# One residual load in mid-run moved mostly to a chosen eleven of the 16 DMA engines, and 15 tiny reads removed, in a memory-bound layer norm

## The chip, the cores and the metric

The kernel runs on one core of a Trainium2 chip. The metric is the device time of one execution in microseconds (us). The profile counts the packets of every queue against the core's 16 DMA engines, which move data between HBM and the on-chip memory (SBUF, 128 partitions); transfers are issued on the sync queue, the scalar queue and GpSimd (queue tables below).

## The reference

```python
# x, residual: (16, 1024, 512) float32; gamma, beta: 512 values
z = x + residual
mean = np.mean(z, axis=-1, keepdims=True)
var = np.var(z, axis=-1, keepdims=True)
return gamma * (z - mean) / np.sqrt(var + eps) + beta
```

Two arrays of 33.5 MB are read and one is written, 100.7 MB in all. There are 16,384 rows; each partition holds 128 of them, and "row" below means one of these 128, across all partitions.

## The kernel before

GpSimd adds x and residual two rows at a time, ScalarE takes mean and variance, VectorE applies two passes. All large transfers go through the sync queue: loads of 8 rows (16 KB per partition), stores of 16 rows (32 KB per partition). A load or store of 128 partitions makes 128 packets, one for each partition (in the trace 4224 packets of 16 KB for 33 transfers of 8 rows), and 16 reports of its landing come, one for each engine; at equal shares that is 8 partitions on each engine.

```python
X_CHUNKS = [8] * 16
R_CHUNKS = [8] * 16
OUT_CHUNKS = [16] * 7 + [8, 4, 4]
Z_ROWS, R_ROWS, STORE_LAG = 64, 32, 40

def load_r(lo, n):
    nc.sync.dma_start(out=part(rbuf, R_ROWS, lo, n), in_=dram(rf, lo, n))
def store(lo, n):
    nc.sync.dma_start(out=dram(of, lo, n), in_=part(zbuf, Z_ROWS, lo, n))
# ... (adds, statistics, affine passes cut)

few = consts.tile([16, 16, 16], FP32)
probes = list(range(15, 0, -1))
def probe():                       # tiny reads of 15, 14, ... 1 rows of 64 bytes
    if probes and asked > 48:
        k = probes.pop(0)
        nc.sync.dma_start(out=few[:k, k, :], in_=xf[:k, :16])

for lo, n in spans(X_CHUNKS):
    asked = lo + n
    load_x(lo, n)
    probe()
    while loads_r and loads_r[0][0] + loads_r[0][1] <= asked:
        while added < loads_r[0][0] + loads_r[0][1] - R_ROWS:
            added, done = next(steps)
        load_r(*loads_r.pop(0))
        probe()
    # ... (broadcast of gamma and beta cut)
    store_due()
```

Of the kernel before, what the change touches and what calls it, by code (L numbers as in the profile page):

```python
# [7 lines left out]
FP32 = mybir.dt.float32  # L8
# [5 lines left out]


X_CHUNKS = [8] * 16
R_CHUNKS = [8] * 16
OUT_CHUNKS = [16] * 7 + [8, 4, 4]

GROUP = 2  # L20

Z_ROWS = 64
R_ROWS = 32
# [5 lines left out]
def kernel(  # L29
# [9 lines left out]
    nc = tc.nc  # L39
    P = nc.NUM_PARTITIONS  # L40
    xf = x.flatten_outer_dims()
    rf = residual.flatten_outer_dims()
    of = out.flatten_outer_dims()
    N, D = xf.shape
# [3 lines left out]
    def spans(sizes):  # L48

        assert sum(sizes) == total  # L50
        return [(sum(sizes[:c]), n) for c, n in enumerate(sizes)]
# [3 lines left out]
    def dram(t, lo, n):  # L55

        k = lo % BLOCK
        assert k + n <= BLOCK
        v = t[P * (lo - k) : P * (lo - k + BLOCK), :].rearrange("(p j) d -> p j d", p=P)
        return v[:, k : k + n, :].rearrange("p a b -> p (a b)")  # L60

    consts = ctx.enter_context(tc.tile_pool(name="consts", bufs=1))
# [14 lines left out]
    rbuf = consts.tile([P, R_ROWS, D], FP32)  # L77

    def part(buf, size, lo, n):
        assert lo % size + n <= size  # L80
        return buf[:, lo % size : lo % size + n, :].rearrange("p a b -> p (a b)")

    def load_x(lo, n):
        nc.sync.dma_start(out=part(zbuf, Z_ROWS, lo, n), in_=dram(xf, lo, n))  # L84

    def load_r(lo, n):
        nc.sync.dma_start(out=part(rbuf, R_ROWS, lo, n), in_=dram(rf, lo, n))  # L87

    def store(lo, n):
        nc.sync.dma_start(out=dram(of, lo, n), in_=part(zbuf, Z_ROWS, lo, n))  # L90
# [19 lines left out]
    groups = []  # L110
    for lo, n in spans(R_CHUNKS):
        for j in range(0, n, GROUP):
# [75 lines left out]
    def spread():  # L188
        for k, dest in ((0, gamma_t), (1, beta_t)):
            nc.tensor.matmul(dest, ones, gb_row[:, k, :], start=True, stop=True)  # L190
# [14 lines left out]
    added = done = asked = 0  # L205
    loads_r = spans(R_CHUNKS)
    stores = spans(OUT_CHUNKS)

    def store_due():
        nonlocal added, done  # L210
        while stores and (
            stores[0][0] + stores[0][1] <= asked - STORE_LAG or asked == total
        ):
            lo, n = stores.pop(0)
            while done < lo + n:
                added, done = next(steps)
            store(lo, n)


    few = consts.tile([16, 16, 16], FP32)  # L220
    probes = list(range(15, 0, -1))

    def probe():
        if probes and asked > 48:
            k = probes.pop(0)
            nc.sync.dma_start(out=few[:k, k, :], in_=xf[:k, :16])

    for lo, n in spans(X_CHUNKS):
        asked = lo + n
        assert not stores or stores[0][0] >= asked - Z_ROWS  # L230
        load_x(lo, n)
        probe()
        while loads_r and loads_r[0][0] + loads_r[0][1] <= asked:

            while added < loads_r[0][0] + loads_r[0][1] - R_ROWS:
                added, done = next(steps)
            load_r(*loads_r.pop(0))
            probe()
        if lo == 0:
            spread()  # L240
        store_due()
# [35 lines left out]
```

## Time and profile before

| | before |
|---|---|
| time, median of 3 | 243.33 us (243.16 to 243.63) |
| span of the profiled run | 241.5 us |
| data moved | 100.76 MB, mean 417 GB/s |
| GpSimd waiting for residual loads | 69.9 us |
| one packet of 16 KB / 32 KB / 8 KB | 611 / 1213 / 309 ns |

From the profile page of the kernel before: the mean busy share of the 16 DMA engines in 40 slices of the span (tenths), what they moved in GB/s in each slice, and the queue table (packets, MB, share of 16 engines' span).

```profile
DMA  7999999999999999999999999999999999999992
GB/s 261 434 434 434 432 427 421 426 419 434 432 449 434 404 429 426 434 425 422 434 430 437 434 426 430 429 442 418 432 421 422 470 400 430 470 434 434 399 410 109
q1 hardware_dynamic: 6288, 100.67, 97.9%
q14 instruction: 10, 0.08, 0.1%
```

The engines are busy from the first slice to the last, so their throughput is the bound. In the last slice, however, they are only two tenths busy on average. From the table of groups, the GpSimd adds (count | busy us, mean ns | idle us before them and what ended it):

```profile
L120 POOL TENSOR_TENSOR zbuf<-zbuf,rbuf 128x1024 f32<-128x1024 f32 x64 | 148.6, 2355 | 71.7 <-DMA rbuf<-in_residual_dram 69.9
```

GpSimd waits for data, not the reverse. The trace also records when each engine reports each transfer as landed. These are the reports of the last store, sorted (us from the start of the span; worked out from the semaphore records):

```
before: 236.78 236.78 236.79 236.81 236.83 236.83 236.90 236.91 236.93 236.95 237.06 237.07 | 237.51 239.25 240.11 240.33
```

Twelve engines finish together near 237, four later, and the last one sets the end. This view does not name the engine; the tiny reads were used for that. Each read of k rows was reported k times. The reports of the last five, again in us:

```
5 rows: 144.79 145.28 145.58 146.91 146.98
4 rows: 149.74 150.21 151.88 152.48
3 rows: 154.65 155.10 157.41
2 rows: 159.60 162.29
1 row:  174.07
```

The 128-partition loads beside them have twelve level reports and four late ones, for example 159.10 to 159.41 and 159.83, 160.09, 161.47, 162.11. From read to read one lag drops out. In this document, engine k is the one that drops out between the read of k+1 rows and that of k, and engine 0 the one that reports the read of one row. So engine 1 is late by 2.7 us in the read of 2 rows, engine 3 by 2.1 in that of 4, engine 4 by 0.8 in that of 5, and engine 2 by 0.5 in that of 3. Engines 5 to 15 are the rest. That every read uses the engines of the next smaller one and one more is inferred from these lags.

### The profile page before, as it was taken

The numbers are of one execution on the slowest core, as the hardware profiler recorded it, in microseconds if no ns is written. First come the engines' busy times: TensorE is split into PE (matmuls) and PEld (weight loads), VectorE is DVE, ScalarE is ACT, GpSimd is POOL, SyncE is SP. The second block draws the span as 40 slices with busy tenths as digits, with TensorE's granted clock in tenths as the row PEclk, the third lists the DMA queues.
The fourth block names the chain that finished last, engine by engine and source line by source line (L and its number), as shares of the span: only waits on it lengthen the run. The fifth ranks groups of instructions, "written<-read, shape, count | busy, mean of one in ns | idle before, by whom it ended". The sixth has DMA issues, their size and how long they took to land.

```text
span 241.5 us, 1302 instructions
## 1 busy us (share of the span) xinstructions
PE 4.1 (2%) x4; PEld 1.0 (0%) x4; DVE 185.3 (77%) x322; ACT 189.8 (79%) x578; POOL 148.8 (62%) x68
## 2 busy tenths in 40 slices
PE   3300000000000000000000000000000000000000
PEld 0000000000000000000000000000000000000000
DVE  0009999999999999999969999099991999729700
ACT  2049999999999999999959996399954999459300
POOL 0089999889998606995068940789408893095000
DMA  7999999999999999999999999999999999999992
GB/s 261 434 434 434 432 427 421 426 419 434 432 449 434 404 429 426 434 425 422 434 430 437 434 426 430 429 442 418 432 421 422 470 400 430 470 434 434 399 410 109
DMA packets 6302, 100.76 MB, mean 417 GB/s; under 512 B 914, under 2 KB 914, under 8 KB 916
## 3 DMA queue, kind: packets, MB, share of 16 engines
q1 hardware_dynamic: 6288, 100.67, 97.9%
q14 instruction: 10, 0.08, 0.1%
q10 hardware_dynamic: 4, 0.00, 0.0%
HBM read 67.12 MB, written 33.55 MB: 417 GB/s over the span
## 4 chain that ended last, share of the span: by engine, by line
DMA 82%; POOL 5%; DVE 5%; issue 1%; SPq 1%; DVEq 0%; POOLq 0%
DMA zbuf<-in_x_dram 39%; DMA rbuf<-in_residual_dram 33%; DMA out_dram<-zbuf 10%; POOL zbuf L120 5%; DVE zbuf L161 2%; DVE zbuf L175 2%; SPq L84 0%; SPq L90 0%; DVEq L272 0%; SPq L87 0%; DVE rstd L173 0%; POOLq L120 0%; DVEq L161 0%
## 5 line engine op out<-in xcount | busy, mean ns | idle before, releaser
L120 POOL TENSOR_TENSOR zbuf<-zbuf,rbuf 128x1024 f32<-128x1024 f32 x64 | 148.6, 2355 | 71.7 <-DMA rbuf<-in_residual_dram 69.9
L161 DVE SCALAR_TENSOR_TENSOR zbuf<-zbuf,nm,gamma_t 128x512 f32<-128x512 f32 x128 | 90.0, 745 | 39.4 <-issue 20.3
L131 ACT ACTIVATE junk<-zbuf 128x512 f32<-128x512 f32 x128 | 74.5, 582 | 32.3 <-POOL zbuf L120 32.3
L175 DVE SCALAR_TENSOR_TENSOR zbuf<-zbuf,rstd,beta_t 128x512 f32<-128x512 f32 x128 | 90.0, 745 | 2.3
L140 ACT ACTIVATE junk<-zbuf,nm 128x512 f32<-128x512 f32 x128 | 86.2, 674 | 0.0
L140 ACT ACTIVATION_READ_ACCUMULATOR junk<-zbuf,nm 128x1 f32 x128 | 24.2, 189 | 0.0
L131 ACT ACTIVATION_READ_ACCUMULATOR junk<-zbuf 128x1 f32 x128 | 24.1, 188 | 0.0
L148 ACT ACTIVATE std<-ssq,eps_t 128x2 f32<-128x2 f32 x64 | 17.0, 266 | 2.1
L173 DVE RECIPROCAL rstd<-std 128x2 f32<-128x2 f32 x64 | 10.5, 165 | 0.0
L186 ACT ACT_TABLE_LOAD x1 | 1.3, 1283 | 1.5 <-PEq L258 1.5
L190 PE MATMUL beta_t<-gb_row,ones 1*128 1x512 f32 x2 | 2.1, 1136 | 2.5 <-DMA gb_row<-in_beta_dram 2.5
L190 PE MATMUL gamma_t<-gb_row,ones 1*128 1x512 f32 x2 | 2.0, 1122 | 2.2 <-DMA gb_row<-in_gamma_dram 2.2
L104 DVE MEMSET ones<- 1x128 f32 x1 | 0.2, 165 | 0.8 <-PEq L258 0.8
L190 PEld LDWEIGHTS beta_t<-gb_row,ones 1*128 1x128 f32 x2 | 0.5, 306 | 4.0 <-DMA gb_row<-in_beta_dram 4.0
L190 PEld LDWEIGHTS gamma_t<-gb_row,ones 1*128 1x128 f32 x2 | 0.5, 308 | 2.2 <-issue 2.2
L258 POOL MEMSET const-float32-0.0<- 128x1 f32 x1 | 0.1, 99 | 0.2 <-issue 0.2
L186 ACT ACTIVATE warm<-eps_t 128x1 f32<-128x1 f32 x1 | 0.2, 203 | 0.0
L258 POOL MEMSET const-bfloat16-1.0<- 128x1 bf16 x1 | 0.1, 102 | 0.0
L258 POOL MEMSET const-uint8-127<- 128x1 uint8 x1 | 0.1, 102 | 0.0
L258 POOL MEMSET const-float32-1.0<- 128x1 f32 x1 | 0.1, 99 | 0.0
L106 DVE MEMSET eps_t<- 128x1 f32 x1 | 0.1, 59 | 0.0
## 6 DMA issues: line engine op xcount, KB each, us to landing
zbuf<-in_x_dram SPq DMA_DIRECT2D x16, 2048.0 KB
rbuf<-in_residual_dram SPq DMA_DIRECT2D x16, 2048.0 KB
out_dram<-zbuf SPq DMA_DIRECT2D x7, 4096.0 KB
out_dram<-zbuf SPq DMA_DIRECT2D x1, 2048.0 KB
out_dram<-zbuf SPq DMA_DIRECT2D x2, 1024.0 KB
gb_row<-in_gamma_dram ACTq DMA_DIRECT2D x1, 2.0 KB
gb_row<-in_beta_dram ACTq DMA_DIRECT2D x1, 2.0 KB
few<-in_x_dram SPq DMA_DIRECT2D x1, 0.9 KB
```

Of the source, the lines that this page charges most:

```text
L104: nc.vector.memset(ones, 1.0)
L106: nc.vector.memset(eps_t, float(eps))
L120: nc.gpsimd.tensor_tensor(out=z, in0=z, in1=part(rbuf, R_ROWS, j0, n), op=ALU.add)
L131: nc.scalar.activation(out=junk, in_=zrow(j0 + k), func=ACT.Identity, scale=-inv_d, accum_out=nm[:, k : k + 1],)
L140: nc.scalar.activation(out=junk, in_=zrow(j0 + k), func=ACT.Square, bias=nm[:, k : k + 1], accum_out=ssq[:, k : k + 1],)
L148: nc.scalar.activation(out=std[:, :n], in_=ssq[:, :n], func=ACT.Sqrt, bias=eps_t[:, 0:1], scale=inv_d,)
L161: nc.vector.scalar_tensor_tensor(out=zrow(j0 + k), in0=zrow(j0 + k), scalar=nm[:, k : k + 1], in1=gamma_t, op0=ALU.add, op1=ALU.mult,)
L173: nc.vector.reciprocal(out=rstd[:, :n], in_=STD.pop(g)[:, :n])
L175: nc.vector.scalar_tensor_tensor(out=zrow(j0 + k), in0=zrow(j0 + k), scalar=rstd[:, k : k + 1], in1=beta_t, op0=ALU.mult, op1=ALU.add,)
L186: nc.scalar.activation(out=warm, in_=eps_t, func=ACT.Sqrt)
L190: nc.tensor.matmul(dest, ones, gb_row[:, k, :], start=True, stop=True)
L258: nc = _bacc.Bacc("TRN2", target_bir_lowering=False, num_devices=1)
```

## The change

The intent is to level the engines: take work from engines 0 to 4, give it to engines 5 to 15, and drop the tiny reads that had served to find out which ones are late.

```diff
-R_CHUNKS = [8] * 16
+R_CHUNKS = [8] * 11 + [4, 4] + [8] * 4
+SPARED = 5
+SPARING_ROW = 88
+    def load_r_sparing(lo, n):
+        rest = 16 - SPARED
+        most = P // rest * rest                      # 121
+        dst, src = part(rbuf, R_ROWS, lo, n), dram(rf, lo, n)
+        for q, p0, p1 in (
+            (nc.gpsimd, most, most + SPARED),        # 5 partitions
+            (nc.gpsimd, 0, most),                    # 121 partitions
+            (nc.sync, most + SPARED, P),             # 2 partitions
+        ):
+            q.dma_start(
+                out=dst[p0:p1, :], in_=src[p0:p1, :], max_dma_last_dim=n * D * 2
+            )
 ... (few, probes and probe() removed, with their two calls)
-            load_r(*loads_r.pop(0))
+            load = load_r_sparing if loads_r[0][0] == SPARING_ROW else load_r
+            load(*loads_r.pop(0))
```

More of the change, by code (lines that the diff above doesn't have):

```diff
@@ L217, in store_due @@
             store(lo, n)
-    few = consts.tile([16, 16, 16], FP32)
-    probes = list(range(15, 0, -1))
-    def probe():
-        if probes and asked > 48:
-            k = probes.pop(0)
-            nc.sync.dma_start(out=few[:k, k, :], in_=xf[:k, :16])
     for lo, n in spans(X_CHUNKS):
@@ L231 @@
         load_x(lo, n)
-        probe()
         while loads_r and loads_r[0][0] + loads_r[0][1] <= asked:
@@ L236 @@
                 added, done = next(steps)
-            load_r(*loads_r.pop(0))
-            probe()
+            load = load_r_sparing if loads_r[0][0] == SPARING_ROW else load_r
+            load(*loads_r.pop(0))
         if lo == 0:
```

## The prediction

> **What bounds it.** DMA throughput. The page's 40 slices show the DMA engines at 9 tenths in every slice but the first and last, and the queue table gives the main queue 97.9% of the 16 engines' span. GpSimd spends 69.9 us waiting for residual loads (view of waits). In the trace a 16 KB packet takes 611 ns, a 32 KB one 1213, an 8 KB one 309. One engine's share is about 234.6 us; data starts at 1.7 us with a slow first packet, so a gapless engine ends near 237.
>
> **The engines are not level.** The trace records when each of the 16 engines reports each transfer. For the last store 12 report at 236.8 to 237.1 us, the others at 237.5, 239.25, 240.1 and 240.3; the span ends at 241.5. Two to three engines set the end. The tiny reads identify them: [...]the reads of 5, 4, 3, 2, 1 rows drop one late reporter at a time: engine 1 is latest (2.7 us at t=160), then 3, 4, 2; engine 0 is about 0.2 late. The lag comes in steps, many beside the ten 8 KB packets of the instruction queue (32 to 203 us); a data packet beside one took 961 to 1456 ns instead of 611 or 1213. I take these for instruction refills on engines 0 to 4.
>
> **What the change does.** An ordinary 4-row load is 8 packets of 8 KB per engine, 2.47 us. Now:
> - GpSimd sends 5 partitions[...], then 121, 11 each on 5 to 15; sync sends the last 2 to engines 0 and 1.
> - Packets become 4 KB, about 157 ns by extrapolation (an estimate). Engines 5 to 15 carry 22, 3.46 us: +1.0. Engines 0 and 1 carry two partitions, 0.63 us: -1.85. Engines 2 to 4: -2.16.
> - Removing 15 tiny reads saves little: engine 0 took all 15 and is at most 0.2 to 0.3 us late, so under 20 ns each; up to 0.25 us on engine 1.
> - GpSimd issues after its 30th add (about 97 us), where it then idles 10 us; two issues of 1 to 2 us (an estimate) hide there. The sync queue runs 6 us or more ahead at the waits I checked, so loads landing 1 to 3 us later cost nothing.
>
> **New ends:** engine 1: 240.33-1.85-0.25 = 238.2; engine 3: 237.7; engine 4: 236.9; engines 5 to 15: 237.07+1.0 plus some switching between queues, 238.1 to 238.5. The end moves from 240.3 to about 238.4, all of it critical: -1.9 us. Perfect balance would give at most about -2.8, so faster by 2% is out of reach.
>
> **Predicted:** 241.4 us, 240.7 to 242.7. Faster by over 2%: 0.02; within 2%: 0.95; slower: 0.03.
>
> **Right if:** the last store's reports lie within about 1.5 us, ending near 238.4; a GpSimd queue appears with some 250 packets of 4 KB near 160 ns; no DMA slice falls below 9.
>
> **Wrong if:** the 121-partition load goes over 16 engines[...]: no relief, about 243.5. Or each switch between GpSimd's and sync's packets costs 0.1 us: engines 5 to 15 gain 2 us more, and the gain is lost. Or refills move. Or the late loads drain the queue.

The sum came to 240.33-1.85-0.25 = 238.2 us for engine 1 and 237.07+1.0 and a little more for engines 5 to 15, so to an end at about 238.4 instead of 240.3, and 243.3-1.9 = 241.4 us. The terms of 1.85, 2.16 and 1.0 us take 11 of the 121 partitions for each of engines 5 to 15 and one of the five for each of engines 0 to 4. That was the assumption. Afterwards the trace of the changed kernel had the reports of the load of 121 in two groups, five at 124.22 to 126.34 us and eleven at 127.57 to 128.24, and two reports of the load of 2 partitions (149.82 and 151.67). Which engine carried which of the five partitions, no trace shows. The 157 ns were an estimate from the 309, 611 and 1213 of the larger packets.

## The result, and the profile after

| | before | after |
|---|---|---|
| time, median of 4 | 243.36 us (243.16 to 243.63) | 245.63 us (245.47 to 245.67) |
| ratio | | 1.0092 (95% interval 1.0074 to 1.0109) |

A ratio here and below is the mean time of one kernel's fast runs over that of the other's of the same rounds, so it is not quite the ratio of the medians. The changed kernel is slower by 2.3 us, where a gain of 1.9 was expected. The same lines of the page after the change:

```profile
DMA  7999999999999999999999999999999999999995
GB/s 259 430 433 430 430 426 430 432 428 430 430 426 430 428 433 430 434 452 327 288 354 430 436 426 421 433 441 430 422 429 425 441 432 422 444 430 430 430 413 238
q1 hardware_dynamic: 6054, 99.63, 97.5%
q0 software_dynamic: 416, 1.03, 1.1%
q14 instruction: 9, 0.07, 0.1%
L139 POOL TENSOR_TENSOR zbuf<-zbuf,rbuf 128x1024 f32<-128x1024 f32 x64 | 148.6, 2354 | 72.1 <-DMA rbuf<-in_residual_dram 66.4
L104 POOL DMA_DIRECT2D rbuf<-in_residual_dram x2 | 1.5, 766 | 0.3 <-POOL zbuf L139 0.3
```

Read the two DMA rows together. The busy share is 9 everywhere, but in three slices the rate falls to 327, 288 and 354 GB/s. GpSimd is not the reason: its two issues took 1.5 us and it still idles 72.1 us. The stretch from 110 to 128 us shows it best. The columns are us of the stretch, busy us (count) of PE, PEld, DVE, ACT and POOL, the clock, the DMA share and GB/s; first the kernel before:

```profile
110.00:128.00 18.00, 0.00 (x0) 0.00 (x0) 15.03 (x27) 15.28 (x49) 7.27 (x4) 1.00 1.00 426
```

and the changed kernel:

```profile
110.00:128.00 18.00, 0.00 (x0) 0.00 (x0) 13.87 (x25) 12.00 (x38) 3.00 (x2) 1.00 1.00 328
```

The engines were fully occupied in both and moved 23% less. The missing 18 us x 98 GB/s is 1.76 MB, or 4.1 us at 427 GB/s. So a packet is in flight for longer. Medians of the packets' durations in the changed kernel, from the trace:

| stretch | sync queue runs | 4 KB packet of GpSimd | 16 KB packet | 32 KB packet |
|---|---|---|---|---|
| 106 to 110 us | stores | 159 ns | | 1213 ns |
| 112 to 118 us | loads | 162 ns | 824 ns | |
| 118 to 120 us | loads | 164 ns (up to 365) | 1004 ns | |
| 128 to 134 us | loads, GpSimd's done | | 615 ns | |

Beside stores, GpSimd's packets cost their own time only. Beside loads, the 16 KB packets grew by a third or more. In 118 to 120 us even the shortest of all 16 KB packets took 815 ns, so the engines that carried few or no GpSimd packets were slowed as well. The last store shows the outcome:

```
after: 239.50 240.06 240.51 241.45 241.61 | 241.62 241.63 241.72 241.74 241.77 241.80 241.82 241.90 242.07 242.33 242.58
```

Compare one earlier transfer, the x load of rows 88 to 95, which stands ahead of the residual rows that were moved. Before, twelve engines reported it at 144.43 to 144.73 us and the late four at 145.10 to 146.79. After, five reported it at 149.17 to 150.94 and eleven at 151.69 to 152.47. The eleven are 7.2 us or more later, of which 22 GpSimd packets of 159 ns on each (the 242 packets of the 121 partitions at equal shares) explain 3.5. The five are over 4 us later as well, though at equal shares only two such packets, 0.3 us, are left for each. Everyone lost nearly 4 us that no packet of theirs explains.

### The profile page after: what moved, and what is told of

It is laid out like the page before. It is cut to its first block, busy times and chain, and to the rows that moved or that the text cites. A ratio compares the mean times of both kernels' runs of the same rounds, so it can differ in the third digit from the quotient of the medians.

```text
span 243.7 us, 1266 instructions
## 1 busy us (share of the span) xinstructions
PE 4.1 (2%) x4; PEld 1.0 (0%) x4; DVE 185.2 (76%) x322; ACT 189.5 (78%) x578; POOL 150.3 (62%) x70
## 5 line engine op out<-in xcount | busy, mean ns | idle before, releaser
L139 POOL TENSOR_TENSOR zbuf<-zbuf,rbuf 128x1024 f32<-128x1024 f32 x64 | 148.6, 2354 | 72.1 <-DMA rbuf<-in_residual_dram 66.4
L209 PE MATMUL gamma_t<-gb_row,ones 1*128 1x512 f32 x2 | 2.0, 1121 | 2.7 <-DMA gb_row<-in_gamma_dram 2.7
L104 POOL DMA_DIRECT2D rbuf<-in_residual_dram x2 | 1.5, 766 | 0.3 <-POOL zbuf L139 0.3
```

The lines of the kernel that those rows point to most:

```text
L104: q.dma_start(out=dst[p0:p1, :], in_=src[p0:p1, :], max_dma_last_dim=n * D * 2)
L139: nc.gpsimd.tensor_tensor(out=z, in0=z, in1=part(rbuf, R_ROWS, j0, n), op=ALU.add)
L209: nc.tensor.matmul(dest, ones, gb_row[:, k, :], start=True, stop=True)
```

## The experiments

**The theory (ports).** The changed kernel's packets grew beside loads (16 KB from 611 to 824 and 1004 ns) and not beside stores (159 and 1213), and in 118 to 120 us all 27 of them took 815 ns or more. Undisturbed, a packet of 16,384 bytes takes 611 ns, 26.8 GB/s. The author's conjecture was that the place in SBUF decides: when the partitions of a load fall on engines otherwise than in a whole load of 128, packets that write at the same time hold each other up. The expectations call this the port theory. No trace shows how the ways into SBUF are divided or which of them an engine uses. It can be tested by what it foretells: that it matters which partitions a load writes, and not which queue sends it or which HBM rows it reads.

**The rivals.** First (queue), that switching between GpSimd's packets and the sync queue's costs some 0.2 us each time: while both queues were active, GpSimd's packets came about 1000 ns apart instead of 611+159=770. The prediction had named this one. Second (HBM), that reading those HBM rows together is slow.

All kernels below start from the changed kernel. Each result is compared with the kernel before, run on the same chip. Where an expectation speaks of the base, e1_sync is meant.

### e1_sync: the tiny reads alone

```diff
-            load = load_r_sparing if loads_r[0][0] == SPARING_ROW else load_r
+            load = load_r
```

> The changed kernel with its 4-row load sent whole on the sync queue, 128 partitions on all 16 engines: only the tiny reads are gone and one 8-row load is cut in two. All theories: about 243.1 us (242.9 to 243.4), at most 0.3 under the kernel before, because engine 0 took 15 tiny reads and was only 0.2 us late. Last store: 11 or more engines level within 0.3 us, two or three 2 to 3.5 us late, as before. It is the base for the runs beside it.

Measured: 243.03 us (before 243.41), ratio 0.9984 (0.9972 to 0.9997). The tiny reads cost about 0.4 us in all (0.1 to 0.7 by the interval; the cut of one load in two is included). The last store: eleven engines at 236.77 to 237.18 (somewhat wider than the 0.3 us expected), then 237.19, 237.44, 238.36, 239.85 and 239.94. So the spared load alone cost the changed kernel 2.6 us.

### e2_gp128: GpSimd, but all 128 partitions in one load

```diff
-        for q, p0, p1 in ( ...three pieces... ): q.dma_start(...)
+        nc.gpsimd.dma_start(out=dst, in_=src, max_dma_last_dim=n * D * 2)
```

> The same 4 rows in one GpSimd load of 128 partitions in 4 KB packets, on all 16 engines. Port theory[...]: [...]no loss: a 16 KB packet beside a 4 KB one is spaced 611+159=770 ns, time 243.1 to 243.8. Queue theory (each GpSimd packet between sync packets costs about 0.2 us, as the spacing of about 1000 ns in the changed kernel suggests): 16 packets per engine lose 3 us, time about 246, spacing about 970 ns again.

Measured: 243.3 us (before 243.41), ratio 0.9997 (0.9984 to 1.0011). In the same stretch, with GpSimd's 4 KB packets between the sync queue's 16 KB packets as in the changed kernel:

```profile
110.00:128.00 18.00, 0.00 (x0) 0.00 (x0) 13.97 (x25) 12.50 (x39) 4.85 (x3) 1.00 0.98 415
```

It moved 415 GB/s, not 328. The medians were 159 ns for 4 KB and 611 to 613 for 16 KB throughout. GpSimd, its queue, the alternation and the 4 KB size are cleared at once; the queue theory falls.

### e3_sp121: the same three pieces without GpSimd

```diff
-            (nc.gpsimd, most, most + SPARED),
-            (nc.gpsimd, 0, most),
+            (nc.sync, most, most + SPARED),
+            (nc.sync, 0, most),
```

> The same three pieces (5, 121 and 2 partitions, 4 KB packets), all on the sync queue: no GpSimd, one queue[...]. Queue theory: imbalance alone, about 244.7 us, packets of 4 KB at 159 ns and 16 KB at 611. Port theory: packets of the window are slow here as well (4 KB well over 159, 16 KB over 611 on engines that work past it), and it loses 1 to 2 us more: 245.5 to 247.

Measured: 250.85 us (before 243.41), ratio 1.0304 (1.0289 to 1.0318). On the sync queue alone the split does far more harm: the 4 KB packets took medians of 320 to 385 ns between 144 and 152 us (in stretches of 2 us), twice their 159, and the few 16 KB packets beside them 1228 to 1272. The direction is the port theory's, but the size was underestimated. At the last store of e3 five engines end at 240.18 to 240.97 and eleven at 243.82 to 247.23. The five lie within 0.8 us, so the two that are 2.7 us late in e1_sync are probably among the eleven that carry more: e3 is not a clean measure of this cost.

### e5_halves: half of the partitions at a time

```diff
+        for p0, p1 in ((0, P // 2), (P // 2, P)):
+            nc.sync.dma_start(
+                out=dst[p0:p1, :], in_=src[p0:p1, :], max_dma_last_dim=n * D * 4
+            )
```

> The same 4 rows as two sync loads of 64 partitions in 8 KB packets, each on all 16 engines, 4 packets per engine: same bytes per engine, same queue[...]. Port theory: the 8 KB packets take about 620 ns instead of 309, the load costs about 2.4 us more, time 245.2 to 246. Queue theory, or any that blames GpSimd or packet size: no loss, 243.0 to 243.5.

Measured: 248.46 us (before 243.41), ratio 1.0215 (1.0199 to 1.0231). The load has the same bytes as in e1_sync, at equal shares the same for every engine, on the same queue. The stretch in which it runs, in e1_sync:

```profile
142.00:152.00 10.00, 0.00 (x0) 0.00 (x0) 8.43 (x15) 6.58 (x22) 2.48 (x2) 1.00 1.01 425
```

and in e5_halves:

```profile
142.00:152.00 10.00, 0.00 (x0) 0.00 (x0) 8.66 (x15) 6.71 (x21) 0.00 (x0) 1.00 1.01 268
```

Equal busy shares, 425 against 268 GB/s. The 8 KB packets took 578 to 620 ns (medians between 146 and 150 us) where 309 is normal, close to the 620 that was expected under the port theory. The loss of 5.4 us over e1_sync is more than the 2.4 that I had reckoned. The packets of neighbouring transfers were slowed too: the few 16 KB packets between 144 and 150 us took 1121 to 1805 ns, and those between 152 and 154 us a median of 1081. How much of the loss that makes was not measured.

### e6_low64, e7_mid64, e8_cross, e9_cross: partitions or HBM rows?

Each adds one redundant load of 64 partitions to the base, into a scratch tile. Two write partitions 0 to 63, two write 32 to 95. The HBM rows that are read are varied independently.

```diff
+    def load_r_extra(lo, n):
+        load_r(lo, n)
+        nc.sync.dma_start(
+            out=scratch[0:64, :], in_=dram(rf, lo, n)[0:64, :]     # e6; e7 has 32:96 twice
+        )                                                          # e8: 0:64 <- 32:96; e9: 32:96 <- 0:64
```

> The base (load whole on sync, no tiny reads) plus one redundant sync load of 64 partitions, 8 KB each, into a scratch tile at partitions 0 to 63. That is 4 packets, 1.24 us, more for every engine. [...]Port theory: well over its bytes, since the two 64-partition loads cost 4.4 us too much together: +3 to +3.7 us over the base of 243.0, so 246 to 246.8; 8 KB packets near 600 ns. Rival (reads of 64 rows at a time are slow in HBM): the same here, and the same in its twin.

> The twin: the same redundant load with partitions and rows 32 to 95[...]. Same number of rows, bytes, packets, engines and queue. Port theory: only its bytes, +1.24 to +1.5 us, so 244.2 to 244.6, 8 KB packets at 309 ns. Rival (HBM rows): as the other, 246 or more.

> The redundant load into scratch partitions 0 to 63[...], but reading the HBM rows of partitions 32 to 95. Port theory: slow, as the run with partitions and rows 0 to 63 (247.8): 246.5 to 249, some 8 KB packets near 700 ns. Rival (the HBM rows read together decide): fast, as the twin with rows 32 to 95 (244.8).

> The redundant load into scratch partitions 32 to 95[...], reading the HBM rows of partitions 0 to 63. Port theory: fast, 244.5 to 245.1, 8 KB packets at 309 ns. Rival (HBM rows): slow, 246.5 to 249.

| SBUF partitions written | HBM rows 0 to 63 | HBM rows 32 to 95 |
|---|---|---|
| 0 to 63 | e6: 247.83 us, ratio 1.0195 (1.0156 to 1.0234) | e8: 247.47 us, 1.0177 (1.0162 to 1.0192) |
| 32 to 95 | e9: 244.85 us, 1.0067 (1.0052 to 1.0082) | e7: 244.82 us, 1.0064 (1.0047 to 1.0081) |

The partitions decide, the HBM rows do not; the HBM theory falls. One load of half a megabyte into partitions 0 to 63 costs 2.6 to 3.0 us more than the same load into 32 to 95. Why these two ranges differ, the runs do not show. The crossed pair in the stretch of the load, e8_cross first:

```profile
144.00:154.00 10.00, 0.00 (x0) 0.00 (x0) 6.54 (x12) 4.59 (x14) 1.98 (x1) 1.00 1.03 338
```

and e9_cross:

```profile
144.00:154.00 10.00, 0.00 (x0) 0.00 (x0) 6.87 (x12) 6.56 (x21) 4.02 (x2) 1.00 1.02 430
```

e6 came out about 1 us above its expectation and varied more than any other run (246.97 to 249.39); e7 was 0.2 us above its own. e8 and e9 met theirs for the port theory.

### v1_store4k: the same idea, as a store

If the conflict is between writes into SBUF, then a spared store should be free of it while the sync queue runs loads. This version keeps all loads whole on sync and splits four rows of one store instead.

```diff
-R_CHUNKS = [8] * 11 + [4, 4] + [8] * 4
-SPARING_ROW = 88
+R_CHUNKS = [8] * 16
+SPARING_ROW = 48
     def store(lo, n):
+        if lo == SPARING_ROW:
+            store_sparing(lo, 4)          # the same three pieces: GpSimd 5 and 121, sync 2
+            lo, n = lo + 4, n - 4
         nc.sync.dma_start(out=dram(of, lo, n), in_=part(zbuf, Z_ROWS, lo, n))
```

> The idea turned round: no tiny reads, all loads whole on sync; of the store of rows 48 to 63, four rows are stored by the same 5, 121 and 2 partition pieces (GpSimd and sync, 4 KB packets), issued near 112 us, in a phase in which the sync queue runs loads. Stores read SBUF and loads write it; in the changed kernel the GpSimd loads cost only their bytes while the sync queue ran stores (106 to 110 us: 159 and 1213 ns). Port theory[...]: no conflict, engines 0 to 4 relieved by about 1.9 us and the others burdened by 1.0: about 241.4 us (240.9 to 242.3). If [...]sparing engines never pays: 244 to 246.

Measured: 241.3 us (241.24 to 241.78; before 243.3), ratio 0.9924 (0.9909 to 0.9938), correct. It beats both kernels. The stretch with GpSimd's packets, and the queues:

```profile
110.00:128.00 18.00, 0.00 (x0) 0.00 (x0) 14.61 (x26) 14.85 (x46) 8.16 (x6) 1.00 1.01 426
q1 hardware_dynamic: 6054, 99.63, 97.7%
q0 software_dynamic: 416, 1.03, 1.1%
```

It has the same number of GpSimd packets as the changed kernel, at 426 GB/s instead of 328, with medians of 159 and 611 ns. The last store:

```
v1_store4k: 236.09 236.27 236.89 | 237.57 237.60 237.61 237.66 237.68 237.75 237.76 237.87 237.88 237.90 238.01 238.04 238.20
```

The last engine ends at 238.20 instead of 240.33. The prediction's sum for the engines (238.2 for engine 1, 238.1 to 238.5 for 5 to 15) is nearly met here, in the version without conflict: the last one fits, and most of the others end up to 0.5 us sooner. One transfer after the split store, five engines report at 129.71 to 130.54 us and eleven at 133.18 to 133.60, so five were indeed spared, and with no engine past 238.20 at the end it fits that the two latest of the kernel before were among them. Of the gain of 0.8%, about 0.2% comes from dropping the tiny reads (e1_sync) and about 0.6% from the split store.

### v1_store8k: packets of 8 KB

```diff
-                out=dst[p0:p1, :], in_=src[p0:p1, :], max_dma_last_dim=n * D * 2
+                out=dst[p0:p1, :], in_=src[p0:p1, :], max_dma_last_dim=n * D * 4
```

> As the last, with the packets at 8 KB, so 11 of them per engine that end sooner. If the 121 partitions again go to engines 5 to 15: the same or 0.2 us faster, 240.9 to 242.0. If without the extra dimension they are spread over 16 engines[...]: no relief of engines 0 to 4, about 243.3; the last store tells which.

Measured: 243.83 us (before 243.3), ratio 1.0023 (1.0008 to 1.0037). The two latest engines stayed late (240.29 and 240.73), and shortly after the split store one engine alone was 1.7 us ahead of the rest (125.53 against 127.23 and later). It would fit 8 partitions on each of 15 engines and one on the last: 7 packets of 309 ns fewer are 2.2 us (an estimate). So the 4 KB form (121 x 2 x 1024) went to eleven engines, and the 8 KB form (121 x 2048) did not. The two differ in packet size and in the extra dimension at once; which of them decides was not tested.

### e13_store_low and e14_store_mid: does it matter where a store reads, too?

The base plus one redundant store of 64 partitions to a scratch in HBM.

```diff
+        if lo == 48:
+            nc.sync.dma_start(
+                out=spare[0:64, :],                                 # e14: 32:96 in both
+                in_=part(zbuf, Z_ROWS, 48, 4)[0:64, :],
+            )
```

> The base plus one redundant sync store of 64 partitions, 8 KB each, from partitions 0 to 63[...] to a scratch in HBM. If SBUF reads are limited[...] as writes are: about +4 us over the base, 246.5 to 248.5, 8 KB packets near 600 to 700 ns. If reads are not so limited: +1.3 to 1.8, 244.3 to 244.9, packets at 309.

> Its twin from partitions 32 to 95[...]: 244.3 to 244.9 under either, packets at 309 ns.

Measured: 245.27 us (before 243.14), ratio 1.009 (1.0072 to 1.0108), and 244.51 us, ratio 1.0051 (1.0036 to 1.0066). The difference of 0.8 us is more than nothing and much less than the 2.6 to 3.0 of the loads; neither expectation for the low half was met. Most 8 KB packets took 309 ns even there; nine between 168 and 173 us took 362 to 1271. So a store from partitions 0 to 63 loses a little against one from 32 to 95. Why the stores suffer so much less than the loads, these runs do not show.

### e10_group4 and v2_group4: fewer instructions

```diff
-GROUP = 2
+GROUP = 4
-            store_sparing(lo, 4)              # v2 only
+            store_sparing(lo, 2)
```

> The base with 4 rows per group instead of 2: 32 GpSimd adds instead of 64, 32 square roots and reciprocals instead of 64, fewer semaphore instructions; the same DMAs. Theory of the late engines (8 KB instruction refills delay the engine they fall on by 0.4 to 1 us each): 1 to 3 fewer refills than the base's 9, the latest two engines 0.5 to 1 us less late at the last store: about 242.3 us (241.9 to 242.8). If the lag has another cause: 243.0. The tail has about 6 us of slack for the longer group.

> The sparing store (no conflict, 241.3 us) with 4 rows per group and only 2 rows stored in the spared way, 2 KB packets, since the engines should be less unequal: engines 5 to 15 burdened by about 0.5 instead of 1.0 us, 0 to 4 relieved by about 1. If the refill theory holds, 240.9 us (240.5 to 241.4); if not, engines 1 and 3 stay late and it is 242.

Measured: 243.02 us, ratio 0.9989 (0.9972 to 1.0005), and 242.81 us, ratio 0.9985 (0.997 to 1.0001). Both missed. Larger groups cut ScalarE's records in the trace from 663 to 599, but the instruction queue still carried 9 packets of 8 KB, only later, and the latest engines stayed as late (239.94 and 240.44). The 0.4 to 1 us of the expectation were the estimate: in the kernel before, nine of the ten packets have a data packet beside them that took 0.24 to 0.66 us longer. The premise, fewer refills, did not come about, so e10 neither supports nor weakens the refill theory; v2 spared less and had as much to level, which fits its being slower than v1.

### e11_pe300, e12_pe150, e15_pool8: what makes engines late?

The whole gain rests on a few late engines. The first two add tiny matmuls on the idle tensor engine, the third adds tiny memsets on GpSimd.

```diff
+        for _ in range(300):                  # e12: 150
+            nc.tensor.matmul(idle, ones, gb_row[:, 0, :8], start=True, stop=True)
+        for k in range(8):                    # e15 instead: after each of the 64 adds
+            nc.gpsimd.memset(idle[:, 8 * g + k : 8 * g + k + 1], 0.0)
```

> The base plus 300 tiny fp32 matmuls on the idle tensor engine (each four instructions in the trace), into a PSUM tile that nobody reads; the DMAs are the same. If refills make engines late: about 9 more 8 KB packets on the instruction queue, all on one engine that was on time before (the earliest now drops out of the level group), 0.35 to 0.9 us each, so it ends 3 to 8 us later than the level 237 and sets the end at 240 to 245: time 243.3 to 248. If they do not: 243.0 as the base.

> Half the dose, 150 matmuls, 4 to 5 more refills. Refill theory: a further engine is late by 1.5 to 4 us at the last store; it may just reach the two that are latest already, so 243.0 to 244.2, and the lag is about half of that with 300. Otherwise: the last store is as in the base, 13 engines near level.

> The base plus 512 tiny memsets on GpSimd (8 after each add, about 0.1 us each, into cells that nobody reads); the DMAs are the same. [...]GpSimd should draw about 4 more 8 KB packets[...], 13 instead of 9. Refill theory: one engine that was 0.3 to 0.5 us late at the last store is 1.5 to 4 us late, each step beside one of the new packets. Rival (the lag has another cause): the new packets come and the last store is as in the base, 13 engines within 0.7 us. Time 243.0 to 244 under either.

Measured: 242.95 us, ratio 1.0007 (0.9971 to 1.0044); 242.87 us, ratio 0.9987 (0.9972 to 1.0002); 243.2 us, ratio 0.9997 (0.9981 to 1.0014). e11 and e12 also cut one PSUM pool (stdp) from 3 buffers to 2 to make room. Two passages of the last expectation were cut earlier; one of them said that the matmuls had drawn no instruction packet. They did draw some, of 16 KB, on a queue of their own. The instruction queues of e1_sync:

```profile
q14 instruction: 9, 0.07, 0.1%
```

of e11_pe300:

```profile
q8 instruction: 4, 0.07, 0.1%
q14 instruction: 9, 0.07, 0.1%
```

of e12_pe150:

```profile
q14 instruction: 9, 0.07, 0.1%
q8 instruction: 2, 0.03, 0.1%
```

and of e15_pool8:

```profile
q14 instruction: 13, 0.11, 0.1%
```

with the last reports of the last store:

```
e1_sync:   237.11 237.18 237.19 237.44 238.36 239.85 239.94
e11_pe300: 238.09 238.42 238.77 238.78 238.79 239.81 239.90
e12_pe150: 237.15 237.33 238.14 239.14 239.43 240.24 240.38
e15_pool8: 237.01 237.08 237.28 238.55 240.00 240.38 240.61
```

The 16 KB packets of queue q8 go with further late engines, one for each: none and three engines past 238 us in e1_sync, two and five in e12, four and seven in e11. They start at 26.4, 53.9, 81.2 and 108.5 us in e11 (26.0 and 53.7 in e12) and take about 1.0 to 1.1 us. The steps come at these times: at the transfer reported near 27 us, one engine is 1.6 us (e11) and 1.8 us (e12) behind the level ones, where e1_sync has none more than 0.3 behind. The form of the expectation was wrong all the same: the packets were fewer and larger and fell on several engines, none of which became the last, so the time stayed.

In e15, four more 8 KB packets of 309 ns go with one more engine that ends at about 240: about 2.6 us more lag for an engine that had stood at 237.44 or earlier, or 0.64 us for each packet. In e1_sync, too, each of the nine packets has a data packet beside it that took 0.16 to 0.66 us longer than usual. That instruction packets delay the DMA engine they fall on is thus shown by two different means, each in one profiled run. How they are assigned to DMA engines, these runs do not show.

## Why the prediction was wrong

- **Bound and critical path: right.** The DMA engines bound the kernel, and the last engine of the last store sets the end. In the runs whose last store is quoted here, the time moved with it.
- **Which engines are late and why: right as far as shown.** The late engines were told apart by the tiny reads (five reports down to one, above); v1_store4k, which spares five engines, takes away the two latest. That instruction packets delay an engine is shown by e11_pe300, e12_pe150 and e15_pool8.
- **"Removing 15 tiny reads saves little": right.** Up to 0.25 us was said; e1_sync measured about 0.4, with an interval that holds both.
- **GpSimd's issues and the depth of the sync queue: right.** The two issues took 1.5 us and no slice of the DMA row between the first and the last fell below 9. The 4 KB packet was taken at 157 ns and took 159.
- **"Engines 5 to 15 carry 22, 3.46 us: +1.0" and "Engines 0 and 1 ... -1.85": this is the step that failed.** The sum counted each engine's own packets and took all other packets to be unchanged. Measured at the x load of rows 88 to 95, the eleven lost about 3.7 us beyond their own packets, and the five about 4, since 16 KB packets took medians of 784 to 1004 ns instead of 611 between 110 and 126 us (in stretches of 2 us). Against the base, the level engines end 4.8 to 5.4 us later instead of 1.0, and the early five 1.6 us or more later than the base's last five, compared in order, instead of 1.9 to 2.2 us sooner.
- **The missing term is where a load writes.** e2_gp128 shows that the same GpSimd packets, in one load of 128 partitions, slow nothing (16 KB packets at 611 to 613 ns); e5_halves (8 KB packets at 578 to 620 ns) and the four crossed loads (2.6 to 3.0 us) show that the partitions written decide. That this is also what slows the spared load is inferred; the trace does not record which partition a packet wrote, or how the ways into SBUF are divided. The HBM rows, too, were varied only for the loads of 64 partitions, not for the spared load.
- **"Wrong if ... each switch between GpSimd's and sync's packets costs 0.1 us":** the symptom was foreseen (packets spaced wider than their sum), the cause was not. e2_gp128 rules the switch out. The warning that 121 partitions might go over 16 engines did not come true for this form, but the reports of v1_store8k fit it for the plainer one.
- **The arithmetic of the engines' own packets was sound.** In v1_store4k, where the split does not conflict, the last engine ended at 238.20, as predicted, and the time was 241.3 against the 241.4 that had been predicted for the changed kernel. So close an agreement is partly luck, since most engines ended up to 0.5 us sooner than the sum had them.

## What to carry to other kernels

When DMA throughput binds, look at when each engine finishes, not at the mean busy share, and count a transfer at both ends: by the engines that carry it and by the partitions that it writes. Here a load that was sent in pieces of 5, 121 and 2 partitions slowed the other loads in flight (16 KB packets from 611 to about 820 ns), and loads of 64 partitions cost 2.6 to 3.0 us more into partitions 0 to 63 than into 32 to 95; the sign is a DMA row at 9 with a falling rate and packets longer than their usual time. Leveling engines can still pay if it is done with a store beside loads: here the split store gained about 0.6%. And every instruction queue of the table has to be read, not only the one that was there before: q8 is easily overlooked.
